# Two chunks of x held in transposed blocks until their rms is known, instead of being read a second time by rows

## The chip, the cores and the metric

One core of one Trainium2 chip. The time is device microseconds (us) of one launch, inputs in HBM to output in HBM. The kernel before takes 2092.69 us, the median of three runs (2089.51 to 2094.95).

## The reference

One decoder layer over x of 2048 positions by 1024 channels, in float32:

```python
h = rmsnorm(x, pre_norm_g)                       # x * rsqrt(mean(x*x over channels) + eps) * g
proj = h @ w_in                                  # 1024 x 8192
u_s, z_s, q, k, v, z_a, g_s, g_a = split(proj)
y_s = s5_branch(u_s, ...) * silu(z_s)
y_a = dilated_attention_branch(q, k, v) * silu(z_a)
merged = sigmoid(g_s) * (y_s @ w_branch_s) + sigmoid(g_a) * (y_a @ w_branch_a)
x = x + rmsnorm(merged @ w_out, post_norm_g)
```

Only the first line and the first use of `h` (the 512 columns of `u_s`) are touched here: the norm needs, for each position, the sum of squares over its 1024 channels.

## The kernel before

**Layout.** The products contract over channels, so the kernel keeps h transposed in SBUF: channels on the partitions in eight blocks of 128 (`k`), positions along the free axis. The 2048 positions are four chunks `q` of 512, so one block is a tile of 128x512 (256 KB). HBM holds x twice: `xT`, by chunk and block, and `x`, by rows. To keep float32 accuracy each operand is split in two float32r halves, `hi` (a ScalarE copy, L67) and `lo` (a VectorE subtraction, L68); `proj` (L132) makes one bank of 128x512 out of 24 matmuls, three for each block.

**The first stage**, `start` (L253), fills `hhi` and `hlo` and makes the four banks of `u` for each chunk (`products(q)`, L260). Two ways of handling the norm stand in it:

- Chunks 0 and 1, `load_raw` (L201): the blocks are loaded, split unscaled (L73, L74), and their squares (ScalarE, L213 and L216) are added up on VectorE (L217). Four small matmuls with a column of ones sum over the partitions (L220). The products run on the unscaled halves, and the scale goes in when a bank is evicted (L268). Later `scale_h` (L244) scales the halves for the rest of the kernel.
- Chunks 2 and 3, `rms` (L223) and then `load_scaled` (L235): the chunk is loaded by rows, four tiles `xr` of 128x1024 (512 KB, two buffers), and ScalarE squares and sums each in one instruction (L232) into `ssr` (one buffer). When the scale is known, the eight transposed blocks are multiplied by gain and scale on VectorE (L241) and split (L67, L68). The products then run on scaled halves and are evicted plainly (L266).

`spread` (L187) turns four columns of sums into the scale: a reciprocal square root out of twelve small VectorE instructions (`rsqrt`, L76, lines 80 to 90), four diagonal tiles (L194), one matmul that broadcasts them over the partitions (`bc`, L196) and a ScalarE copy into `bs` (L198, three buffers). An evicted bank `ue` goes through one of two `ev` buffers to HBM (L270).

**Order.** The program is written in the order of lines 272 to 285. The framework then fixes one order of instructions for each engine when the kernel is built, out of the program's order and a simulated timeline; on the chip each engine follows that order and waits where an operand is late. SyncE issues all these loads and stores. The blocks `xT` have seven buffers, which `scale_h` shares (its tile `ht`).

Of the kernel before, what the change touches and what calls it, by code (L numbers as in the profile page):

```python
# [11 lines left out]
F32 = mybir.dt.float32  # L12
F32R = mybir.dt.float32r
I32 = mybir.dt.int32
AF = mybir.ActivationFunctionType
ALU = mybir.AluOpType
# [3 lines left out]
D_MODEL = 1024  # L20
# [7 lines left out]
TABS = ((0, 16), (16, 16), (32, 16), (48, 16), (64, 9), (73, 9), (82, 16), (98, 16), (114, 16), (130, 16), (146, 16))  # L28
TAB_R8, TAB = 162, 163
SXB = 5  # L30


H_PAD, SHIFT = 56, 72
# [2 lines left out]
def raw(ap):  # L36
    return ap.bitcast(F32)


class Builder:  # L40
# [146 lines left out]
    def spread(self, ss, pool, psum):  # L187
# [10 lines left out]
        nc.scalar.activation(bs, bc, AF.Copy)  # L198
        return bs

    def load_raw(self, q, pool, psum, wp=None, w=None):  # L201

        nc = self.nc
        sl = slice(q * 512, (q + 1) * 512)
        acc = pool.tile([128, 512], F32, tag="xsq", name="acc", bufs=3)
        for k in range(8):
            if w and k % 2 == 0:
                self.strip(wp, w, 0, 0, slice(k, k + 2), 1)
            x = pool.tile([128, 512], F32, tag="xT", name="xT", bufs=7)
            nc.sync.dma_start(x, self.a["xT"][q, k])  # L210
            self.split(self.hhi[:, k, sl], self.hlo[:, k, sl], x, self.gpre[:, k : k + 1])
            if k == 0:
                nc.scalar.activation(acc, x, AF.Square)  # L213
            else:
                sq = pool.tile([128, 512], F32, tag="xsq", name="xsq", bufs=3)
                nc.scalar.activation(sq, x, AF.Square)  # L216
                nc.vector.tensor_tensor(acc, acc, sq, op=ALU.add)  # L217
        ss = psum.tile([128, 4], F32, tag="s", name="ss")
        for b in range(4):
            nc.tensor.matmul(ss[:, b : b + 1], acc[:, b * 128 : (b + 1) * 128], self.ones[:, 0:1], start=True, stop=True)  # L220
        return self.spread(ss, pool, psum)

    def rms(self, q, pool, psum):  # L223

        nc = self.nc
        ss = pool.tile([128, 4], F32, tag="ssr", name="ssr")
        for b in range(4):
            x = pool.tile([128, D_MODEL], F32, tag="xr", name="xr", bufs=2)
            row = q * 512 + b * 128
            nc.sync.dma_start(x, self.a["x"][row : row + 128])  # L230
            unused = pool.tile([128, D_MODEL], mybir.dt.bfloat16, tag="xsq", name="unused", bufs=3)
            nc.scalar.activation(unused, x, AF.Square, accum_out=ss[:, b : b + 1])  # L232
        return self.spread(ss, pool, psum)

    def load_scaled(self, q, bs, pool):  # L235
        nc = self.nc
        sl = slice(q * 512, (q + 1) * 512)
        for k in range(8):
            x = pool.tile([128, 512], F32, tag="xT", name="xT", bufs=7)
            nc.sync.dma_start(x, self.a["xT"][q, k])  # L240
            nc.vector.scalar_tensor_tensor(x, x, self.gpre[:, k : k + 1], bs, op0=ALU.mult, op1=ALU.mult)  # L241
            self.split(self.hhi[:, k, sl], self.hlo[:, k, sl], x)

    def scale_h(self, q, bs, pool):  # L244
        sl = slice(q * 512, (q + 1) * 512)
        for k in range(8):
            hi, lo = self.hhi[:, k, sl], self.hlo[:, k, sl]
            t = pool.tile([128, 512], F32, tag="xT", name="ht", bufs=7)
            self.nc.vector.tensor_tensor(t, raw(hi), raw(lo), op=ALU.add)
            self.nc.vector.tensor_tensor(t, t, bs, op=ALU.mult)  # L250
            self.split(hi, lo, t)

    def start(self, wp, pool, ev, psum):  # L253


        nc = self.nc
        us = [self.pair_tiles(wp) for _ in range(2)]
        back = lambda t: t.rearrange("p (s i) -> p s i", s=4)[:, ::-1]

        def products(q, scale=None):  # L260
            for ct in range(4):
                ps = psum.tile([128, 512], F32, tag=("proj", "n", "t")[(4 * q + ct) // 2 % 3], name="proj")
                self.proj(ps, us[ct // 2], ct % 2, self.pos(q))
                e = ev.tile([128, 4, 128], F32, tag="ev", name="ue")
                if scale is None:
                    nc.scalar.activation(e, back(ps), AF.Copy)  # L266
                else:
                    nc.vector.tensor_tensor(e, back(ps), back(scale), op=ALU.mult)  # L268
                s0 = 4 - 4 * (q % 2)
                nc.sync.dma_start(self.ud[ct * 128 : (ct + 1) * 128, s0 : s0 + 4, q // 2], e)  # L270

        b0 = self.load_raw(0, pool, psum, wp, us[0])
        for ct in range(1, 4):
            self.strip(wp, us[ct // 2], ct % 2, ct)
        b1 = self.load_raw(1, pool, psum)
        products(0, b0)
        b2 = self.rms(2, pool, psum)
        self.load_scaled(2, b2, pool)
        b3 = self.rms(3, pool, psum)
        self.load_scaled(3, b3, pool)  # L280
        products(1, b1)
        products(2)
        self.scale_h(0, b0, pool)
        self.scale_h(1, b1, pool)
        products(3)
# [178 lines left out]
    def ssm_pair(self, g0, pool, psum, tabd, kd):  # L464
# [68 lines left out]
        def rotation():  # L533
# [3 lines left out]
            c, s = (pool.tile(sh, F32, name=n) for n in ("rot_c", "rot_s"))  # L537
            t = pool.tile(sh, F32, tag="sx", name="rot_t", bufs=SXB)
            w = pool.tile(sh, F32, tag="sx", name="rot_w", bufs=SXB)
            g = nc.gpsimd  # L540
# [8 lines left out]
        def wide_tile():  # L549
            return pool.tile([128, 2, 256], F32, tag="sx", name="sx", bufs=SXB)  # L550

# [52 lines left out]
        def gelu():  # L604

            py = m["py"].rearrange("p g x -> p (g x)")
            v = pool.tile([128, 512], F32, tag="sx", name="gv", bufs=SXB)
            nc.scalar.activation(v, py, AF.Square)
# [686 lines left out]
```

## Time and profile before

| | |
|---|---|
| three runs | 2089.51, 2092.69 (median), 2094.95 us |
| the profiled execution | 2096.55 us, its span 2094.7 us |
| TensorE (PE) busy | 2049.4 us, 98% of the span |
| VectorE (DVE), ScalarE (ACT), GpSimd (POOL) busy | 903.0, 592.3, 397.8 us |
| read from HBM, written | 146.52 MB, 74.56 MB |

The profile is of one execution. PE is matmul, PEld its weight loads, SPq the issue of a DMA on SyncE. All times inside the profile count from the start of its span. A busy share tells how much of a time an engine worked, and not whether it was waited for; that is told by the idle time ahead of an instruction and what released it.

### The profile page before, as it was taken

The page shows a single profiled execution, that of the slowest core. Times are in us where ns is not written, and L with a number is a line of the kernel's source. Part 1 is how long each engine was busy: PE and PEld are TensorE (multiplying, and loading weights), DVE is VectorE, ACT ScalarE, POOL GpSimd, SP SyncE. Part 2 cuts the span into 40 slices and gives each one's busy share as a digit, 9 for nine tenths or more (in the row PEclk, how much of TensorE's full clock was granted, in tenths as well). Part 3 has the DMA queues.
Part 4 walks back from the last instruction along what each step waited for, and adds up shares of the span by engine and source line. Part 5 has one row for each costly group of instructions (what it writes and reads, how often), then busy time and mean ns, then how long its engine had stood idle before and what let it go on. Part 6 is the DMA issues. An engine that isn't in the chain of part 4 may idle for free.

```text
span 2094.7 us, 30801 instructions
## 1 busy us (share of the span) xinstructions
PE 2049.4 (98%) x11668; PEld 1786.1 (85%) x11668; DVE 903.0 (43%) x2261; ACT 592.3 (28%) x1327; POOL 397.8 (19%) x384
## 2 busy tenths in 40 slices
PE   8999999999999999999999999999889999999998
PEld 6788888999999988888888888887777887999997
DVE  6881355555442234324424423434311226544434
ACT  6421122222223234334434333432111124112111
POOL 0002355555521200000000000001636101111111
PEclk9999999999999999999999999999999999999999
DMA  7333333333445421111111121113757246433323
GB/s 247 116 115 140 103 115 113 118 114 113 117 121 174 152 67 57 56 61 51 61 56 56 37 66 51 61 52 118 223 157 230 88 136 201 138 125 116 117 81 101
DMA packets 208372, 231.50 MB, mean 111 GB/s; under 512 B 24864, under 2 KB 142944, under 8 KB 207968
## 3 DMA queue, kind: packets, MB, share of 16 engines
q1 hardware_dynamic: 208224, 229.54, 34.9%
q8 instruction: 91, 1.49, 0.3%
q14 instruction: 57, 0.47, 0.1%
HBM read 146.52 MB, written 74.56 MB: 106 GB/s over the span
## 4 chain that ended last, share of the span: by engine, by line
PE 86%; DMA 7%; DVE 2%; ACT 1%; POOL 1%; issue 1%; SPq 0%; DVEq 0%; ACTq 0%; POOLq 0%
PE proj L141 46%; PE pv L163 13%; PE po L1108 8%; PE br L1089 8%; DMA cf<-fd 2%; PE glu L786 2%; PE s L914 2%; PE nb L940 1%; DMA raw<-in_wout_dram 1%; PE na L940 1%; PE nc L978 1%; PE py L598 1%; POOL cn L1030 1%; PE s L970 1%; PE pd L561 1%
## 5 line engine op out<-in xcount | busy, mean ns | idle before, releaser
L141 PE MATMUL proj<-hhi,w_hi 128*128 128x512 f32 x1664 | 664.6, 400 | 25.4 <-ACT ge L693 15.6
L141 PE MATMUL proj<-hlo,w_hi 128*128 128x512 f32 x1664 | 658.2, 396 | 3.3 <-DVE hlo L68 2.7
L141 PE MATMUL proj<-hhi,w_lo 128*128 128x512 f32 x1664 | 657.5, 395 | 0.0
L141 PEld LDWEIGHTS proj<-hhi,w_hi 128*128 128x128 f32 x1664 | 314.5, 189 | 95.0 <-ACT ge L693 18.4
L141 PEld LDWEIGHTS proj<-hlo,w_hi 128*128 128x128 f32 x1664 | 314.3, 189 | 71.3 <-DVE hlo L74 3.2
L141 PEld LDWEIGHTS proj<-hhi,w_lo 128*128 128x128 f32 x1664 | 314.3, 189 | 64.8
L163 PE MATMUL pv<-w_hi,hhi 128*128 128x256 f32 x768 | 218.8, 285 | 0.0
L163 PE MATMUL pv<-w_hi,hlo 128*128 128x256 f32 x768 | 214.5, 279 | 0.0
L163 PE MATMUL pv<-w_lo,hhi 128*128 128x256 f32 x768 | 214.5, 279 | 0.0
L68 DVE TENSOR_TENSOR w_lo<-w_raw,w_hi 128x512 fp32r<-128x512 f32 (+1 forms) x130 | 107.9, 854 | 195.8 <-ACT w_hi L67 195.3
L163 PEld LDWEIGHTS pv<-w_hi,hhi 128*128 128x128 f32 x768 | 144.5, 188 | 0.6
L163 PEld LDWEIGHTS pv<-w_lo,hhi 128*128 128x128 f32 x768 | 144.4, 188 | 0.6
L163 PEld LDWEIGHTS pv<-w_hi,hlo 128*128 128x128 f32 x768 | 144.4, 188 | 0.0
L898 ACT ACTIVATE p<-p,nm 128x256 f32<-128x256 f32 (+1 forms) x192 | 89.5, 467 | 151.8 <-DVE nm L897 135.7
L892 DVE CUSTOM_DVE_ANT_0 p<-s,mask 128x256 f32<-128x256 f32 (+1 forms) x192 | 68.2, 376 | 147.1 <-PE t L973 68.8
L1092 POOL TENSOR_TENSOR gt<-gt 128x256 f32<-128x256 f32 x64 | 48.7, 763 | 390.6 <-DVE gt L1091 224.7
L67 ACT ACTIVATE w_hi<-w_raw 128x512 fp32r<-128x512 f32 (+1 forms) x130 | 76.9, 620 | 111.3 <-DMA w_raw<-in_wst_dram 72.4
L848 POOL CAST kh<-kh 128x128 fp32r<-128x128 f32 x12 | 3.6, 296 | 538.2 <-PE s L970 426.3
L1108 PE MATMUL po<-wout0h,mh 128*128 128x512 f32 x256 | 99.6, 394 | 3.3 <-ACT wout0h L67 3.3
L1108 PE MATMUL po<-wout0l,mh 128*128 128x512 f32 x256 | 100.3, 392 | 0.0
L1108 PE MATMUL po<-wout0h,ml 128*128 128x512 f32 x256 | 100.2, 393 | 0.0
L693 ACT ACTIVATE ge<-proj 128x512 f32<-128x512 f32 x64 | 37.8, 594 | 205.7 <-PE proj L141 134.3
(248 smaller groups left out, 3342.1 us busy)
## 6 DMA issues: line engine op xcount, KB each, us to landing
w_raw<-in_wst_dram SPq DMA_DIRECT2D x126, 256.0 KB
vd<-ve SPq DMA_DIRECT2D x48, 256.0 KB
numd<-acc SPq DMA_DIRECT2D x48, 256.0 KB
cn<-numd SPq DMA_DIRECT2D x48, 256.0 KB
cf<-fd SPq DMA_DIRECT2D x48, 256.0 KB
xT<-in_xT_dram SPq DMA_DIRECT2D x32, 256.0 KB
gts<-ge SPq DMA_DIRECT2D x32, 256.0 KB
sx<-sx SPq DMA_DIRECT2D x64, 128.0 KB
```

The costliest lines, as they stand in the source:

```text
L67: nc.scalar.activation(hi, src, AF.Copy)
L68: nc.vector.tensor_tensor(lo, src, raw(hi), op=ALU.subtract)
L141: last = nc.tensor.matmul(ps, st[:, k, cs], m, start=n == 0, stop=n == 23)
L163: last = nc.tensor.matmul(ps[:, o], st[:, k, rs], m[:, k], start=n == 0, stop=n == 23)
L786: nc.tensor.matmul(ps, st[:, k, cs], m[:, k], start=n == 0, stop=n == 11)
L892: nc.vector.tensor_tensor_reduce(p[:, :n], scores, mask, scale=1.0, scalar=-3.0e38, op0=ALU.add, op1=ALU.max, accum_out=st[:, 0, blk : blk ...
L898: nc.scalar.activation(p[:, :n], p[:, :n], AF.Exp, scale=HEAD_SCALE, bias=nm, accum_out=st[:, 1, blk : blk + 1])
L914: nc.tensor.matmul(s[:, h], x[:, b], y[:, k0 : k0 + 2], start=n == 0, stop=n == 2)
L940: nc.tensor.matmul(out, x, y[:, i0 : i0 + 2], start=n == 0, stop=n == 2)
L1089: nc.tensor.matmul(ps, st[:, k, cs], m[:, i, k], start=n == 0, stop=n == 11)
L1092: nc.gpsimd.tensor_tensor(gt[:, 0], gt[:, 0], gt[:, 1], op=ALU.add)
L1108: nc.tensor.matmul(po[b, half], st[:, k, bs], m[:, k, hs], start=k == 0 and n == 0, stop=k == 7 and n == 2,)
```

## The change

The loads by rows, `rms` and `load_scaled` are gone. `load_held` loads a chunk's eight transposed blocks and keeps them, takes the sum of squares as `load_raw` does (squares on ScalarE, additions on VectorE, four matmuls with ones, now the helper `column_sums`), and `split_held` then scales and splits the same blocks in place. The blocks `xT` get 11 buffers instead of seven. In SBUF the two go even: two tiles `xr` of 4 KB a partition leave, four of 2 KB come.

```diff
+XTB = 11
...
+    def column_sums(self, acc, psum):
+        ss = psum.tile([128, 4], F32, tag="s", name="ss")
+        for b in range(4):
+            block = acc[:, b * 128 : (b + 1) * 128]
+            self.nc.tensor.matmul(ss[:, b : b + 1], block, self.ones[:, 0:1], start=True, stop=True)
+        return ss
...
-    def rms(self, q, pool, psum):
-
-        nc = self.nc
-        ss = pool.tile([128, 4], F32, tag="ssr", name="ssr")
-        for b in range(4):
-            x = pool.tile([128, D_MODEL], F32, tag="xr", name="xr", bufs=2)
-            row = q * 512 + b * 128
-            nc.sync.dma_start(x, self.a["x"][row : row + 128])
-            unused = pool.tile([128, D_MODEL], mybir.dt.bfloat16, tag="xsq", name="unused", bufs=3)
-            nc.scalar.activation(unused, x, AF.Square, accum_out=ss[:, b : b + 1])
-        return self.spread(ss, pool, psum)
-
-    def load_scaled(self, q, bs, pool):
-        nc = self.nc
+        return self.spread(self.column_sums(acc, psum), pool, psum)
+
+    def load_held(self, q, pool, psum):
+
+        nc = self.nc
+        xs = []
+        acc = pool.tile([128, 512], F32, tag="xsq", name="acc", bufs=3)
+        for k in range(8):
+            x = pool.tile([128, 512], F32, tag="xT", name="xT", bufs=XTB)
+            nc.sync.dma_start(x, self.a["xT"][q, k])
+            xs.append(x)
+            if k == 0:
+                nc.scalar.activation(acc, x, AF.Square)
+            else:
+                sq = pool.tile([128, 512], F32, tag="xsq", name="xsq", bufs=3)
+                nc.scalar.activation(sq, x, AF.Square)
+                nc.vector.tensor_tensor(acc, acc, sq, op=ALU.add)
+        return xs, self.spread(self.column_sums(acc, psum), pool, psum)
+
+    def split_held(self, q, xs, bs):
         sl = slice(q * 512, (q + 1) * 512)
-        for k in range(8):
-            x = pool.tile([128, 512], F32, tag="xT", name="xT", bufs=7)
-            nc.sync.dma_start(x, self.a["xT"][q, k])
-            nc.vector.scalar_tensor_tensor(x, x, self.gpre[:, k : k + 1], bs, op0=ALU.mult, op1=ALU.mult)
+        for k, x in enumerate(xs):
+            self.nc.vector.scalar_tensor_tensor(x, x, self.gpre[:, k : k + 1], bs, op0=ALU.mult, op1=ALU.mult)
             self.split(self.hhi[:, k, sl], self.hlo[:, k, sl], x)
...
         products(0, b0)
-        b2 = self.rms(2, pool, psum)
-        self.load_scaled(2, b2, pool)
-        b3 = self.rms(3, pool, psum)
-        self.load_scaled(3, b3, pool)
+        for q in (2, 3):
+            self.split_held(q, *self.load_held(q, pool, psum))
         products(1, b1)
         products(2)
         self.scale_h(0, b0, pool)
```

## Rows read from the trace of the kernel before

**Rows 1.** The page, part 1: busy time, share of the span, instructions

```profile
PE 2049.4 (98%) x11668; PEld 1786.1 (85%) x11668; DVE 903.0 (43%) x2261; ACT 592.3 (28%) x1327; POOL 397.8 (19%) x384
```

**Rows 2.** Busy time by stretch: PE, PEld, DVE, ACT, POOL, PEclk, DMA share, GB/s

```profile
0.00:68.00 68.00, 55.14 (x221) 40.97 (x222) 44.07 (x121) 39.39 (x69) 0.85 (x7) 1.00 0.66 217
...
20.00:40.00 20.00, 20.00 (x92) 16.32 (x92) 12.12 (x32) 11.80 (x21) 0.00 (x0) 1.00 0.70 232
...
40.00:62.00 22.00, 19.65 (x82) 14.93 (x80) 11.46 (x53) 6.42 (x13) 0.00 (x0) 1.00 0.56 168
...
68.00:1400.00 1332.00, 1332.00 (x7803) 1170.69 (x7804) 593.85 (x1464) 414.03 (x956) 244.54 (x233) 1.00 0.29 90
```

**Rows 3.** Timeline of PE, 5 to 68 us: start, us, instruction [idle before, releaser]

```profile
5.57 0.80 PE L141 MATMUL proj<-hhi,w_hi 128*128 128x512 f32 x1 [5.57 <-ACT hhi L73]
...
18.24 0.95 PE L220 MATMUL ss<-ones,acc 128*128 128x1 f32 x8
...
49.36 1.10 PE L196 MATMUL bc<-diag,ones 128*128 128x512 f32 x2 [1.28 <-DVE rs_y L82]
...
62.70 1.10 PE L196 MATMUL bc<-diag,ones 128*128 128x512 f32 x2 [1.77 <-DVE diag L194]
...
67.85 0.50 PE L141 MATMUL proj<-hlo,w_hi 128*128 128x512 f32 x1 [2.70 <-DVE hlo L68]
```

**Rows 4.** Timeline of ACT, 38 to 49 us

```profile
38.05 1.06 ACT L232 ACTIVATE unused<-xr 128x1024 bf16<-128x1024 f32 x1 [3.80 <-DMA xr<-in_x_dram]
...
40.38 0.58 ACT L198 ACTIVATE bs<-bc 128x512 f32<-128x512 f32 x1
...
48.47 1.06 ACT L232 ACTIVATE unused<-xr 128x1024 bf16<-128x1024 f32 x1 [7.51 <-DVE rs_v L80]
```

**Rows 5.** Timeline of DVE, 40 to 63 us

```profile
40.99 1.29 DVE L268 TENSOR_TENSOR ue<-proj,bs 128x512 f32<-128x512 f32 x2 [6.01 <-ACT bs L198]
...
46.76 0.69 DVE L268 TENSOR_TENSOR ue<-proj,bs 128x512 f32<-128x512 f32 x1 [3.34 <-DMA ud<-ue]
...
48.23 0.16 DVE L80 TENSOR_SCALAR rs_v<-ssr 128x4 f32<-128x4 f32 x1
...
51.71 0.88 DVE L194 TENSOR_SCALAR diag<-ident,inv 128x128 f32<-128x128 f32 x4
...
62.47 4.72 DVE L241 SCALAR_TENSOR_TENSOR xT<-xT,gpre,bs 128x512 f32<-128x512 f32 x7
```

**Rows 6.** Timeline of SP: issues of loads, 30 to 70 us

```profile
30.08 0.38 SPq L240 DMA_DIRECT2D xT<-in_xT_dram  x1
...
32.68 1.40 SPq L230 DMA_DIRECT2D xr<-in_x_dram  x2
...
67.82 1.53 SPq L240 DMA_DIRECT2D xT<-in_xT_dram  x3
```

**Rows 7.** Groups by line, 0 to 230 us: busy us, mean ns

```profile
L232 ACT ACTIVATE unused<-xr 128x1024 bf16<-128x1024 f32 x8 | 8.4, 1053 | 15.6 <-DMA xr<-in_x_dram 7.9 <-DVE rs_v L80 7.5
...
L216 ACT ACTIVATE xsq<-xT 128x512 f32<-128x512 f32 x14 | 8.5, 618 | 0.5 <-DVE acc L217 0.4
...
L217 DVE TENSOR_TENSOR acc<-acc,xsq 128x512 f32<-128x512 f32 x14 | 9.6, 685 | 0.0
...
L241 DVE SCALAR_TENSOR_TENSOR xT<-xT,gpre,bs 128x512 f32<-128x512 f32 x16 | 11.0, 745 | 0.0
...
L68 DVE TENSOR_TENSOR hlo<-xT,hhi 128x512 fp32r<-128x512 f32 x16 | 10.2, 686 | 0.7 <-ACT hhi L67 0.7
```

**Rows 8.** Chain that ended last, in order of time: start, us, what

```profile
1.65 3.06 DMA xT<-in_xT_dram
...
67.85 140.83 PE proj L141 x620
```

**Rows 9.** Timelines of DVE and ACT at 88 and 89 us

```profile
88.31 0.69 DVE L68 TENSOR_TENSOR hlo<-xT,hhi 128x512 fp32r<-128x512 f32 x1
...
89.08 0.60 ACT L266 ACTIVATE ue<-proj 128x512 f32<-128x512 f32 x1 [1.22 <-PE proj L141]
```

More of the change, by code (lines that the diff above doesn't have):

```diff
@@ L217, in load_raw @@
                 nc.vector.tensor_tensor(acc, acc, sq, op=ALU.add)
-        ss = psum.tile([128, 4], F32, tag="s", name="ss")
-        for b in range(4):
-            nc.tensor.matmul(ss[:, b : b + 1], acc[:, b * 128 : (b + 1) * 128], self.ones[:, 0:1], start=True, stop=True)
-        return self.spread(ss, pool, psum)
-    def rms(self, q, pool, psum):
-        nc = self.nc
-        ss = pool.tile([128, 4], F32, tag="ssr", name="ssr")
-        for b in range(4):
-            x = pool.tile([128, D_MODEL], F32, tag="xr", name="xr", bufs=2)
-            row = q * 512 + b * 128
-            nc.sync.dma_start(x, self.a["x"][row : row + 128])
-            unused = pool.tile([128, D_MODEL], mybir.dt.bfloat16, tag="xsq", name="unused", bufs=3)
-            nc.scalar.activation(unused, x, AF.Square, accum_out=ss[:, b : b + 1])
-        return self.spread(ss, pool, psum)
-    def load_scaled(self, q, bs, pool):
-        nc = self.nc
+        return self.spread(self.column_sums(acc, psum), pool, psum)
+    def load_held(self, q, pool, psum):
+        nc = self.nc
+        xs = []
+        acc = pool.tile([128, 512], F32, tag="xsq", name="acc", bufs=3)
+        for k in range(8):
+            x = pool.tile([128, 512], F32, tag="xT", name="xT", bufs=XTB)
+            nc.sync.dma_start(x, self.a["xT"][q, k])
[8 more added lines that the diff above has]
+    def split_held(self, q, xs, bs):
         sl = slice(q * 512, (q + 1) * 512)
-        for k in range(8):
-            x = pool.tile([128, 512], F32, tag="xT", name="xT", bufs=7)
-            nc.sync.dma_start(x, self.a["xT"][q, k])
-            nc.vector.scalar_tensor_tensor(x, x, self.gpre[:, k : k + 1], bs, op0=ALU.mult, op1=ALU.mult)
+        for k, x in enumerate(xs):
+            self.nc.vector.scalar_tensor_tensor(x, x, self.gpre[:, k : k + 1], bs, op0=ALU.mult, op1=ALU.mult)
             self.split(self.hhi[:, k, sl], self.hlo[:, k, sl], x)
@@ L247, in scale_h @@
             hi, lo = self.hhi[:, k, sl], self.hlo[:, k, sl]
-            t = pool.tile([128, 512], F32, tag="xT", name="ht", bufs=7)
+            t = pool.tile([128, 512], F32, tag="xT", name="ht", bufs=XTB)
             self.nc.vector.tensor_tensor(t, raw(hi), raw(lo), op=ALU.add)
```

## The prediction, made before the changed kernel was run

> **What bounds the kernel now.** I read the page's busy times first. TensorE is busy for 2049.4 us of a span of 2094.7 [rows 1]: whatever shortens this kernel has to take idle time, or work, away from TensorE. Next the busy time by stretch, to see where that idle time lies [rows 2]. From 68 to 1400 us TensorE is busy for all of 1332 us, and the chain of waits runs over TensorE alone from 67.85 us, 620 matmuls of `proj` in 140.83 us, 0.227 us each [rows 8]. So a microsecond that the first 68 us gain or lose goes straight through to the end: behind them stands a line of matmuls without a hole. In the first 68 us TensorE is busy for 55.14 us and idle for 12.86 us [rows 2]. That is the whole stake.
>
> The timeline of TensorE says what the 12.86 us are [rows 3]. The first 5.57 us are the wait for the first block, which the change doesn't touch. Three more waits are large: 1.28 us ahead of the matmul that broadcasts chunk 1's scale, 1.77 us ahead of chunk 3's, and 2.70 us for the first `lo` half of chunk 2. Together they are 5.75 us; what is left, 12.86 - 5.57 - 5.75 = 1.54 us, is small waits in the first 20 us.
>
> Then I asked why the scales come late, on ScalarE and VectorE. ScalarE stood still for 3.80 us until rows of chunk 2 landed, and the copy `bs` of chunk 0, which needs no rows, stood behind them in ScalarE's order until 40.38 us [rows 4]. The first eviction on VectorE waited 6.01 us for this copy, a later one 3.34 us for a store to free an `ev` buffer [rows 5]. Chunk 2's reciprocal square root stands behind those evictions, so it starts at 48.23 us, though ScalarE was done with chunk 2's rows when it made that copy at 40.38; ScalarE's next square, the first of chunk 3, waits 7.51 us for the root's first step, since `ssr` has one buffer [rows 4, 5]. VectorE reaches chunk 2's first scaled block at 62.47 us. Call this time T; TensorE's wait of 2.70 us follows from it.
>
> **The change, part by part.**
>
> *Removed.* Eight row loads of 512 KB with their issues on SyncE [rows 6]; eight squares with sums on ScalarE, 8 x 1.053 = 8.4 us [rows 7]; the single buffer `ssr`; and the point at which rows block ScalarE ahead of chunk 0's copy. TensorE executed none of it.
>
> *Added on ScalarE.* 16 squares of a block, 16 x 0.618 = 9.9 us [rows 7], 1.5 us more than leaves. ScalarE is busy for 6.42 of the 22 us from 40 to 62 [rows 2], so I cost it at nothing; without that cover it is 1.5 us.
>
> *Added on VectorE.* 14 additions x 0.685 = 9.6 us [rows 7]. VectorE is idle for 7.9 us of 20 to 40 and 10.5 us of 40 to 62 [rows 2], and chunk 2's additions, 4.8 us, fall there. Chunk 2's scaling and splitting, 8 x (0.745 + 0.686) = 11.4 us [rows 7], moves forward into the same idle time. Cost zero on TensorE while it fits; if it does not, the ends to take are zero and 9.6 us.
>
> *Added on TensorE.* Two sets of small matmuls with ones at 0.95 us [rows 3]: 1.9 us. This is paid in full, since there is no hole to hide it in.
>
> *Moved: T.* The seventh block of chunk 2 is issued at 30.08 us already; the eighth has to wait until 67.82 us for a buffer [rows 6]. With 11 buffers it follows at about 30.5 us, and lands 0.38 + 3.06 us later [rows 6, 8], at 33.9 us. Then a square (0.62), an addition (0.69), the sums (0.95), the reciprocal square root to the end of the diagonals (48.23 to 52.59, 4.36 us), the broadcast (1.10) and the copy (0.58) [rows 3, 4, 5, 7] come to 8.3 us. So T is 42.2 us at the earliest, and at the latest the 62.47 us of now. I take 47, near the lower end: of what lies between, the waits for rows and for `ssr` go, while a store's wait like the 3.34 us and two evictions (1.3 us) can still stand ahead.
>
> *The wait that the change adds.* Chunk 2 holds eight of 11 blocks, so five blocks of chunk 3 can be loaded only when a `lo` of chunk 2 frees theirs; chunk 3's scale now hangs on chunk 2's split. Queued behind these loads on SyncE are stores of `u`, behind the squares on ScalarE the `hi` copies. After the last `lo` of chunk 2, T + 11.4, come load (3.4), square and addition (1.3), sums (0.95), the root (4.36), broadcast and copy (1.7): chunk 3's scale is there at T + 23.2 and its last `lo` at T + 34.6, which is 81.6 us. Before, that `lo` started at 88.31 us, and the last bank of chunk 2 was evicted at 89.08 [rows 9]. A bank takes 24 x 0.227 = 5.45 us, and its last block is read 4.8 us in, at 93.9; with the gain below, 91.8. There are 10 us to spare, so I cost this at nothing.
>
> *The three waits.* The 2.70 us go, since chunk 2 is split before TensorE wants it (about 60 us). The 1.28 us go, since chunk 0's copy no longer stands behind rows. The 1.77 us I leave in: chunk 3's chain is still the last and got longer, and a broadcast that follows a small chain is what waited. The new sums may wait too; the nearest rows are the broadcasts' waits, 0 to 1.77 us each [rows 3], and I take 0, nearest to the existing sums, which sit between matmuls without a wait worth a row.
>
> **The sum** is -2.70 - 1.28 + 1.9 = -2.1 us. The profiled execution took 2096.55 us, 3.9 us above the median of 2092.69; the sum comes off either. **Forecast: 2090.6 us**, -0.1%. A measurement of this kernel can tell about 0.3%, 6.3 us, from no change.
>
> **A rule that speaks against the change.** The change takes away DMA and ScalarE time and gives TensorE work, though TensorE is the engine at 98% [rows 1]. The Trainium skill, Perfetto Trace Analysis, section Identifying the Most-Contended Engine, says to optimize the engine of highest occupancy first; taken alone it would leave only the 1.9 us here. The trace disagrees for this stage, where TensorE waited 5.75 us on others. The case itself is the first rival.
>
> **Rivals.**
>
> *The waits form again.* The orders are fixed at build time, and a broadcast or a sum stands in TensorE's order wherever the simulated timeline put it. The three waits come back elsewhere, at the same 5.75 us, and the sums add 1.9: 2094.6 us. For it: four scales and now four sums hang on chains of small VectorE instructions, and VectorE gets fuller. Against: the 2.70 us come from T alone, which moves by 15 us.
>
> *Chunk 3 in lockstep: slower.* Its place is ScalarE's order. If the five late squares stand between chunk 2's `hi` copies, each waits for a load that waits for a `lo`, and the next copy waits behind it. A round is `lo` 0.69, issue 0.38, landing 3.06, square 0.62, copy about 0.62, together 5.4 us in place of 1.43; five rounds add 19.7 us. Chunk 3's last `lo` falls at 101.3 us instead of 81.6, 9.5 us after TensorE wants it, and -2.1 + 9.5 = +7.4 gives 2100.1 us. It costs from the point at which chunk 3 is over 10 us late. For it: the 3.80 us with an unrelated copy behind them are this very pattern [rows 4]. Against: in program order chunk 2's split stands ahead of chunk 3's loads. That ScalarE takes its queue strictly in order is in the Trainium skill, TensorE: Matmul & The Clock Gate, section Architectural detail; [rows 4] agree.
>
> *Everything goes.* All 5.75 us and the 1.54 us of small waits, since the early loads no longer share the DMA queue with rows: -7.3 + 1.9 = -5.4, 2087.3 us. Against: none of the waits of TensorE that have a row was released by a load [rows 3].
>
> **How the numbers follow.** The forecast 0.47, waits form again 0.20, lockstep 0.20, everything goes 0.13. The range runs from 2087.3 less half the spread of the runs (2.7), 2084.5, to the lockstep, 2100.5. Faster by over 0.3% is below 2086.4, which even the best case reaches only with the spread's help: 0.10. Slower by over 0.3% is above 2099.0, most of the lockstep: 0.16. Within: 0.74.
>
> **What would show it.** Right: T near 47 us; TensorE idle in the first 68 us down from 12.86 to about 9; no wait for a `lo` at chunk 2; two more rows of four sums at 0.95 us; still no hole from the first product of chunk 2 to 1400 us. Wrong: T above 57 us, TensorE waiting for chunk 3's `lo`, ScalarE idle for DMA between `hi` copies, or holes past 68 us, where the sum puts none.

## The result, and the profile of the changed kernel

The changed kernel takes 2121.29 us, the median of four runs (2120.79 to 2122.2), beside 2091.64 us for the kernel before on the same chip: a ratio of 1.0138, 95% interval 1.0123 to 1.0153. The forecast was 2090.6 us and its range ended at 2100.5. The profiled execution took 2122.2 us and its span is 2120.4, beside 2094.7 before, so 25.7 us of span have to be found. (The medians are 29.7 us apart; the profiled execution of the kernel before was 4.9 us above its median.)

The page of the changed kernel, busy time, share of the span and instructions, answers to [rows 1]:

```profile
PE 2062.1 (97%) x11684; PEld 1795.0 (85%) x11684; DVE 914.5 (43%) x2275; ACT 594.6 (28%) x1327; POOL 399.9 (19%) x384
```

The busy shares are those of before to a point. TensorE has 16 instructions more, the new sums, and is busy for 12.7 us longer; the sums explain 1.9 of that.

To place the loss I took a landmark, the first matmul of the next stage (`pk`). The kernel before reaches it at 208.51 us, the changed one at 234.09:

```profile
234.09 0.51 PE L509 MATMUL pk<-tab,q 128*128 128x16 f32 x4
```

That is 25.6 us, the whole difference of the spans. So between these two executions nothing is lost or won behind the first stage, and only the first 234 us need reading. Busy time by stretch of the changed kernel (columns as in [rows 2]):

```profile
0.00:68.00 68.00, 55.86 (x228) 42.46 (x229) 49.32 (x117) 37.90 (x65) 0.85 (x7) 0.96 0.54 175
...
68.00:100.00 32.00, 24.06 (x99) 19.37 (x98) 31.45 (x62) 13.07 (x22) 0.00 (x0) 0.87 0.24 74
...
100.00:110.00 10.00, 3.50 (x5) 1.67 (x6) 8.50 (x19) 4.47 (x8) 0.00 (x0) 0.50 0.02 5
...
100.00:150.00 50.00, 41.00 (x160) 31.99 (x161) 41.27 (x183) 15.49 (x26) 0.00 (x0) 0.83 0.33 101
...
150.00:1400.00 1250.00, 1250.00 (x7420) 1102.36 (x7419) 514.61 (x1207) 378.63 (x885) 247.14 (x233) 1.00 0.28 88
```

TensorE's first 68 us hardly changed: idle for 12.14 us, against 12.86 before. The chain that ended last, in order of time (answers to [rows 8]), has the unbroken run of matmuls from 113.16 us, where before it was from 67.85:

```profile
113.16 121.09 PE proj L142 x524
```

The loss lies where the kernel before had no hole at all: 7.94 us idle between 68 and 100, 9.00 between 100 and 150. Idle time of TensorE in the first 150 us is 29.1 us, 16.2 more than before. In the same stretches the granted clock is below 1, down to 0.50 between 100 and 110, which is the lower of TensorE's two levels, 1.2 GHz of 2.4. And VectorE, 43% busy over the span, worked for 31.45 of the 32 us from 68 to 100. The waits of TensorE from 0 to 250 us (waited for, us in total, times, longest):

```profile
PE bc L197 <- DVE diag L195: 12.3, 1, 12.3
PE proj L142 <- ACT hhi L74: 6.7, 2, 5.8
PE proj L142 <- DVE hlo L69: 5.2, 2, 2.7
PE proj L142 <- ACT hhi L68: 4.3, 2, 2.1
```

One wait is three quarters as long as all the extra idle time: 12.3 us for the diagonals of chunk 3's scale. The second row is the first load and was there before. TensorE's timeline (answers to [rows 3]):

```profile
51.98 1.02 PE L197 MATMUL bc<-diag,ones 128*128 128x512 f32 x2
52.83 0.95 PE L206 MATMUL ss<-ones,acc 128*128 128x1 f32 x8
...
59.42 1.02 PE L197 MATMUL bc<-diag,ones 128*128 128x512 f32 x2
62.58 1.84 PE L142 MATMUL proj<-hhi,w_hi 128*128 128x512 f32 x4 [2.13 <-ACT hhi L68]
67.16 0.80 PE L142 MATMUL proj<-hlo,w_hi 128*128 128x512 f32 x1 [2.74 <-DVE hlo L69]
67.75 0.63 PE L142 MATMUL proj<-hhi,w_lo 128*128 128x512 f32 x1
...
85.96 0.95 PE L206 MATMUL ss<-ones,acc 128*128 128x1 f32 x8
...
104.37 2.08 PE L197 MATMUL bc<-diag,ones 128*128 128x512 f32 x2 [12.31 <-DVE diag L195]
108.58 2.08 PE L142 MATMUL proj<-hhi,w_hi 128*128 128x512 f32 x4 [2.13 <-ACT hhi L68]
113.16 0.80 PE L142 MATMUL proj<-hlo,w_hi 128*128 128x512 f32 x1 [2.50 <-DVE hlo L69]
```

The rows are, in this order, chunk 1's broadcast, chunk 2's sums and broadcast, then chunk 3's sums and broadcast. The last two broadcasts are each followed by the same pair of waits: 2.1 us until the scale is copied and the first block is scaled and copied, then 2.5 to 2.7 us until the first `lo` is there. Behind both pairs the matmuls run at half speed for a while: 12 of them from 67.75 us and eight from 113.75 start 0.427 us apart, where 0.227 is the rule.

The cause is one engine further back. VectorE's timeline of the changed kernel (answers to [rows 5]):

```profile
61.11 5.39 DVE L248 SCALAR_TENSOR_TENSOR xT<-xT,gpre,bs 128x512 f32<-128x512 f32 x8 [0.80 <-ACT bs L199]
66.42 4.89 DVE L69 TENSOR_TENSOR hlo<-xT,hhi 128x512 fp32r<-128x512 f32 x8
71.23 0.68 DVE L242 TENSOR_TENSOR acc<-acc,xsq 128x512 f32<-128x512 f32 x1
71.84 1.89 DVE L256 TENSOR_TENSOR ht<-hhi,hlo 128x512 f32<-128x512 f32 x3
...
88.13 0.15 DVE L81 TENSOR_SCALAR rs_v<-ss 128x4 f32<-128x4 f32 x1
88.20 1.28 DVE L257 TENSOR_TENSOR ht<-ht,bs 128x512 f32<-128x512 f32 x2
89.41 0.16 DVE L83 TENSOR_SCALAR rs_y<-rs_v 128x4 int32<-128x4 int32 x1
89.48 0.68 DVE L69 TENSOR_TENSOR hlo<-ht,hhi 128x512 fp32r<-128x512 f32 x1
...
101.57 0.15 DVE L91 SCALAR_TENSOR_TENSOR inv<-rs_t,rs_n 128x4 f32<-128x4 f32 x1
...
103.45 0.86 DVE L195 TENSOR_SCALAR diag<-ident,inv 128x128 f32<-128x128 f32 x4
...
107.11 5.39 DVE L248 SCALAR_TENSOR_TENSOR xT<-xT,gpre,bs 128x512 f32<-128x512 f32 x8 [0.81 <-ACT bs L199]
112.42 4.89 DVE L69 TENSOR_TENSOR hlo<-xT,hhi 128x512 fp32r<-128x512 f32 x8
```

Read the tile names. The tile `ht` belongs to `scale_h`, which rescales chunks 0 and 1 for stages that come much later. Its steps of 0.68 us stand between chunk 3's additions, and again between the twelve small steps of chunk 3's square root: 24 of them between 88.13 us and the diagonals at 103.45, one every 0.60 us. The root and its diagonals take 16.2 us. VectorE waits for nothing there, so the list of waits leads to the diagonals and no further; VectorE is busy with work that nobody needs yet, while TensorE stands still for the one small chain in its midst.

**The account of the 25.6 us**: 16.2 us more idle time; 1.9 us for the new sums; and half-speed work, 20 matmuls x 0.200 = 4.0, the broadcast 2.08 - 1.10 = 1.0, two groups of four at 1.84 and 2.08 where 1.20 is the full-speed time (it stands in a row further down) = 1.5, together 6.5 us. The sum is 24.6; 1.0 us is left over.

**The kernel before had a small case of this already.** This is VectorE's timeline in its trace at chunk 3's root, which no row ahead of the prediction shows:

```profile
57.62 0.16 DVE L87 TENSOR_TENSOR rs_t<-rs_y 128x4 f32<-128x4 f32 x1
57.69 1.28 DVE L268 TENSOR_TENSOR ue<-proj,bs 128x512 f32<-128x512 f32 x2
58.89 0.15 DVE L88 TENSOR_TENSOR rs_t<-rs_t,rs_v 128x4 f32<-128x4 f32 x1
...
61.68 0.87 DVE L194 TENSOR_SCALAR diag<-ident,inv 128x128 f32<-128x128 f32 x4
```

Two evictions stand between two steps of the root. In that kernel the root was over at 62.55 us, ahead of `scale_h`, whose first step came at 82.2. Now the busy time of the kernel before from 68 to 100 us (columns as in [rows 2]):

```profile
68.00:100.00 32.00, 32.00 (x142) 26.48 (x143) 31.30 (x52) 13.26 (x23) 0.00 (x0) 1.00 0.39 124
```

VectorE was full there before the change too, 31.30 of 32 us. The change pushed chunk 3's whole chain into that stretch.

### The profile page after: what moved, and what is told of

Its sections match the earlier page's. It is cut to its first block, busy times and chain, and to the rows that moved or that the text cites. A ratio compares the mean times of both kernels' runs of the same rounds, so it can differ in the third digit from the quotient of the medians.

```text
span 2120.4 us, 30842 instructions
## 1 busy us (share of the span) xinstructions
PE 2062.1 (97%) x11684; PEld 1795.0 (85%) x11684; DVE 914.5 (43%) x2275; ACT 594.6 (28%) x1327; POOL 399.9 (19%) x384
## 4 chain that ended last, share of the span: by engine, by line
PE 90%; DMA 5%; DVE 3%; POOL 1%; ACT 1%; issue 0%; SPq 0%; DVEq 0%; POOLq 0%; ACTq 0%
PE proj L142 49%; PE pv L164 13%; PE po L1113 8%; PE br L1094 8%; DMA cf<-fd 2%; PE glu L791 2%; PE s L919 2%; PE nb L945 1%; PE na L945 1%; DMA cn<-numd 1%; PE nc L983 1%; PE py L603 1%; POOL cn L1035 1%; PE s L975 1%; PE pd L566 1%; PE py L602 1%
## 5 line engine op out<-in xcount | busy, mean ns | idle before, releaser
L69 DVE TENSOR_TENSOR w_lo<-w_raw,w_hi 128x512 fp32r<-128x512 f32 (+1 forms) x130 | 113.7, 897 | 218.4 <-ACT w_hi L68 218.1
L903 ACT ACTIVATE p<-p,nm 128x256 f32<-128x256 f32 (+1 forms) x192 | 89.5, 467 | 148.7 <-DVE nm L902 132.4
```

The costliest lines, as they stand in the source:

```text
L69: nc.vector.tensor_tensor(lo, src, raw(hi), op=ALU.subtract)
L903: nc.scalar.activation(p[:, :n], p[:, :n], AF.Exp, scale=HEAD_SCALE, bias=nm, accum_out=st[:, 1, blk : blk + 1])
```

## The experiments

All compute everything. In the edits, `issue_after(x)` queues what the block issues on the engine of x behind x in that engine's order; it adds no wait between engines. The ratio is to the kernel before on the same chip. "Landmark" is the start of the first `pk` matmul in the profiled execution. Behind it the profiled executions take 1876.8 to 1886.3 us, though no edit touches the later stages, so the landmark shows the first stage without that scatter.

| version | median us (runs) | ratio, 95% interval | landmark us |
|---|---|---|---|
| before | 2091.64 to 2093.21 | 1 | 208.51 |
| the change | 2121.29 (4) | 1.0138, 1.0123 to 1.0153 | 234.09 |
| A. both rescalings queued | 2098.2 (10) | 1.0034, 1.0021 to 1.0046 | 214.31 |
| B. one rescaling queued | 2105.36 (4) | 1.0064, 1.0044 to 1.0084 | 220.39 |
| C. chunk 3's blocks read twice | 2103.79 (4) | 1.0067, 1.0046 to 1.0087 | 224.19 |
| D. only chunk 2 held | 2095.34 (10) | 1.0016, 1.0003 to 1.0029 | 212.26 |
| E. only chunk 3 held | 2098.65 (6) | 1.0036, 1.0022 to 1.0050 | 216.62 |
| F. before, rescalings queued | 2092.32 (10) | 1.0003, 0.9989 to 1.0017 | 207.36 |
| G. A and lagged scaling | 2095.53 (10) | 1.0023, 1.0013 to 1.0033 | 210.28 |
| H. A and evictions queued | 2099.59 (6) | 1.0045, 1.0028 to 1.0062 | 219.47 |
| I. A, lag and evictions | 2091.7 (10) | 1.0008, 0.9998 to 1.0017 | 208.68 |
| J. I and an order on TensorE | 2093.7 (12) | 1.0006, 0.9995 to 1.0016 | 210.46 |

**A. Both rescalings queued behind chunk 3's last split on VectorE.** Nothing else in the program differs from the change; the framework plans the orders of all engines anew.

```diff
+        with self.tc.issue_after(last.ins):
             self.scale_h(0, b0, pool)
             self.scale_h(1, b1, pool)
```

> The changed kernel, with the two scalings of chunks 0 and 1 (scale_h) queued on VectorE behind chunk 3's last split; loads, buffers and sums are as changed. Theory A (the steps of scale_h that the planner puts between the steps of chunk 3's root stretch it from 4.4 to 16 us, and TensorE's wait of 12.3 us for the broadcast hangs on that): the root takes 4 to 5 us again, the 12.3 us wait goes, and with it the two waits of 2.1 and 2.5 us behind it and the slow matmuls that follow them; 2097 to 2103 us. Theory B (the five blocks of chunk 3 that wait for buffers come too late, whatever the order): the broadcast is still waited for by 8 us or more; 2113 to 2122 us.

2098.2 us: 23 of the 30 us come back through an order alone, and 19.8 of the 25.6 us at the landmark. VectorE at chunk 3's root in this kernel:

```profile
79.76 0.16 DVE L81 TENSOR_SCALAR rs_v<-ss 128x4 f32<-128x4 f32 x1 [4.08 <-PE ss L206]
...
82.01 0.87 DVE L195 TENSOR_SCALAR diag<-ident,inv 128x128 f32<-128x128 f32 x4
```

The root with its diagonals takes 3.1 us in place of 16.2, and the broadcast, at 87.67 us, waits for nothing. Three waits of TensorE are left: 2.13 us for chunk 2's first `hi`, then 3.38 and 2.36 us for the first `lo` of chunks 2 and 3 (the last had been expected to go). The loads and the work on every engine are those of the change, so neither the DMA traffic nor the additions by themselves are what cost 23 us. TensorE's order moved too: chunk 3's sums stand at 78.78 us in place of 85.96. A alone therefore can't separate the length of the root from its start; B can.

**B. Only one of the two rescalings queued**, for a dose in between.

```diff
         self.scale_h(0, b0, pool)
-        self.scale_h(1, b1, pool)
+        with self.tc.issue_after(last.ins):
+            self.scale_h(1, b1, pool)
```

> The changed kernel with only one of the two rescalings (scale_h of chunk 1) queued behind chunk 3's last split on VectorE; that of chunk 0 is left as free as it was. Theory A (steps of scale_h that stand between the root's small steps on VectorE make chunk 3's scale late): eight pairs of steps of chunk 0 are left, most of them are used up between chunk 3's additions, so that about three to five stand between the root's steps. The root with its diagonals then takes 5 to 8 us in place of 16, the broadcast of chunk 3 starts at 94 to 97 us in place of 104.4, and the time is 2107 to 2113 us, between that of the order alone (2098) and that of the change (2121). Rival: it is not the steps between, but that the root begins late, at 88 us; then the root begins at the same place and the time stays within 3 us of 2121. Rival 2: any one of the two rescalings is free of cost, and the time is that of the order alone, 2098.

2105.36 us, 1.6 below the band expected of theory A, 13 below the first rival's band and 7 above the second rival's time. The broadcast, expected at 94 to 97 us, starts at 92.31. VectorE's timeline at the root:

```profile
87.27 0.15 DVE L81 TENSOR_SCALAR rs_v<-ss 128x4 f32<-128x4 f32 x1
87.34 0.68 DVE L258 TENSOR_TENSOR ht<-ht,bs 128x512 f32<-128x512 f32 x1
...
91.38 0.87 DVE L195 TENSOR_SCALAR diag<-ident,inv 128x128 f32<-128x128 f32 x4
```

and TensorE's behind it:

```profile
92.31 1.13 PE L197 MATMUL bc<-diag,ones 128*128 128x512 f32 x2 [0.51 <-DVE diag L195]
95.57 1.59 PE L142 MATMUL proj<-hhi,w_hi 128*128 128x512 f32 x4 [2.13 <-ACT hhi L68]
```

This is the cleanest pair with the change: the root begins 0.9 us from where it began there, but three steps of `ht` stand in it instead of 24, and it takes 5.0 us instead of 16.2. TensorE's wait for the diagonals falls from 12.31 to 0.51 us. So the length of the root, and not its late start alone, is what TensorE waited for. The rest, 6.1 us at the landmark between A and B, goes with the start, still 7.5 us behind A: 3.3 us more of waits, and most of what is left is more matmuls at half speed.

**C. Chunk 3 squared from blocks that are not kept, and read a second time for the split.** Its loads no longer hang on chunk 2's split.

```diff
-        for q in (2, 3):
-            self.split_held(q, *self.load_held(q, pool, psum))
+        self.split_held(2, *self.load_held(2, pool, psum))
+        _, b = self.load_held(3, pool, psum)
+        self.load_scaled(3, b, pool)
```

> The changed kernel, but chunk 3's squares are taken from blocks that are let go at once, and the blocks are loaded a second time for the split, so that its sums wait for no buffer of chunk 2. Theory A: scale_h's steps still stand between the root's steps, so the root still takes 13 us or more, but it begins some 20 us earlier and ends before TensorE is through with chunk 2's products; the 12.3 us wait is under 3 us; 2097 to 2105 us. Theory B: the wait goes too, 2097 to 2103 us. A third theory, that the added sums themselves (additions and small matmuls) cost the time wherever they stand: 2113 us or more.

2103.79 us, which rules out the third theory; theories A and B expected nearly the same time. The rescalings are not queued here, and the root is the longest of all, but starts 19 us earlier. VectorE's timeline:

```profile
69.08 0.15 DVE L81 TENSOR_SCALAR rs_v<-ss 128x4 f32<-128x4 f32 x1
...
88.61 0.88 DVE L195 TENSOR_SCALAR diag<-ident,inv 128x128 f32<-128x128 f32 x4
```

and TensorE's:

```profile
92.86 1.02 PE L197 MATMUL bc<-diag,ones 128*128 128x512 f32 x2
96.28 1.20 PE L142 MATMUL proj<-hhi,w_hi 128*128 128x512 f32 x4 [2.40 <-ACT hhi L68]
102.66 0.79 PE L142 MATMUL proj<-hlo,w_hi 128*128 128x512 f32 x1 [5.19 <-DVE hlo L69]
```

The root takes 20.4 us (chunk 2's eight `lo` stand in it beside the steps of `ht`) and TensorE does not wait for it, since it is over by 89.5. So there are two conditions: a root in the midst of filler, and one that starts late. The late start has causes of its own in the change. One is the five blocks of chunk 3 that wait for a free buffer. SyncE's timeline in the changed kernel (answers to [rows 6]):

```profile
67.13 2.73 SPq L235 DMA_DIRECT2D xT<-in_xT_dram  x5
```

The first goes out behind chunk 2's first `lo`, at 67.13 us. C is still 15.7 us behind the kernel before at the landmark. TensorE waits 6.3 us ahead of chunk 2's products, and 2.40 and 5.19 us ahead of chunk 3's, whose scalings begin at 94.81 us, after the broadcast, and whose first `lo` comes at 101.91, behind eight scalings and three more steps of `ht`.

**D and E. Only one of the two chunks held**, the other by rows as before (nine buffers for the blocks, one for the rows, so that SBUF holds both).

```diff
-        for q in (2, 3):
-            self.split_held(q, *self.load_held(q, pool, psum))
+        self.split_held(2, *self.load_held(2, pool, psum))
+        b = self.rms(3, pool, psum)
+        self.load_scaled(3, b, pool)
```

> Chunk 2 held, chunk 3 by rows as before (nine block buffers and one row buffer, to fit). If chunk 3's place behind chunk 2's buffers is the cause, chunk 2's half of the change costs its sums, 0.9 us, and what slow matmuls follow its waits, up to 3 us: 2091 to 2097 us. If holding a chunk costs by itself: half of the 30 us, 2103 to 2109 us.

> Chunk 2 by rows as before, chunk 3 held (nine block buffers and one row buffer). Chunk 3's blocks wait for chunk 2's buffers here too, and scale_h's steps stand between the additions and the root's steps in VectorE's order: if these two are the cause, TensorE waits for chunk 3's broadcast by 8 us or more, 2110 to 2124 us. If holding a chunk costs by itself: 2103 to 2109 us.

D takes 2095.34 us, as expected, E 2098.65. E misses what was expected of it by over 11 us. Its trace agrees with the mechanism, though: in E the framework put only five steps of `ht` between the root's first step and the diagonals, and the root takes 5.8 us (81.24 to 87.07). TensorE's waits there are 2.14 us for the diagonals, 2.91 and 3.11 behind it. Over the 3.1 us of A, the roots of B, E and the change (three, five and 24 steps) are longer by 0.54 to 0.63 us for each step. The two parts of the change lose 0.16% and 0.36% by themselves and 1.38% together; they don't add up. The filler that lands in the root, five steps here and 24 there, is a result of the whole order; the fewer buffers of D and E may have a part in it, which no run separates.

**F. The kernel before with the same queueing as A.**

> The kernel before with the same queue alone: scale_h behind chunk 3's last split on VectorE. There the root of chunk 3 is through before any step of scale_h is ready, so by theory A (the steps between the root's steps) the queue has nothing to win: the first 150 us stay as they are, 2090 to 2095 us. If queueing scale_h late is a gain or a loss of its own, which would then be part of what the same queue did for the changed kernel: outside 2088 to 2097 us.

2092.32 us, no difference that can be told. The rescalings did not harm the kernel before, so what A gains is a repair of something the change brought.

**G, H, I. What is left after A.** G lets `split_held` scale block k only behind the `lo` of block k - 2; in the change all eight scalings stand ahead of the first `lo` (61.11 and 107.11 us). H queues chunk 1's evictions behind chunk 2's last split. I does both.

```diff
+            with self.tc.issue_after(lo[k - 2].ins) if k >= 2 else nullcontext():
                 self.nc.vector.scalar_tensor_tensor(x, x, self.gpre[:, k : k + 1], bs, ...)
...
+        with self.tc.issue_after(first.ins):
             products(1, b1)
```

> The changed kernel with scale_h queued as before, and in each split the scaling of block k queued on VectorE behind the lo of block k-2, in place of eight scalings and then eight subtractions. The first lo comes 3 us earlier (some 63.5 us instead of 66.8), so the wait of 3.4 us for it goes to under 1 us, chunk 3's wait of 2.4 us likewise, and chunk 2's buffers come free from then on: 2093 to 2097 us. If TensorE only meets the next block too late instead (1.43 us of VectorE for a block against 0.68 us of matmuls in one bank), the wait is split over the blocks and nothing is won: 2097 to 2100 us.

> The changed kernel with scale_h queued as before, and the evictions of chunk 1's products queued on VectorE behind chunk 2's last split. Chunk 2's root then follows chunk 1's directly instead of standing behind two evictions that wait for chunk 1's scale and for a store: the first scaled block (61.5 us now) at 55 to 57 us, the waits of 2.1 and 3.4 us ahead of chunk 2 down to 1 to 2 us, and with less waiting no slow matmuls: 2092 to 2096 us. If the place of the evictions doesn't set that time, or the evictions held back stop TensorE for want of a bank: 2098 us or more.

> All three orders together: scale_h behind chunk 3's split, chunk 1's evictions behind chunk 2's split, and scaling and subtraction by turns. Chunk 2's first lo at about 58 us, before TensorE is through with chunk 1 (60 us): no wait above 1 us between 20 and 200 us, no slow matmul after the first 15 us. What is left against the kernel before is -5.75 us of waits and +1.9 us of sums: 2087 to 2091 us. If a cost of holding the blocks is left that no order takes away: 2094 us or more.

G, 2095.53 us, removes both waits for a `lo`; two waits of 2.13 and 2.14 us for a first `hi` stay. H gains nothing over A, 2099.59 us, a miss: its first scaled block comes at 61.34 us, not at 55 to 57, it keeps the bunched scalings, and its waits for `lo` are 3.84 and 3.36 us. I, 2091.7 us, is back at the time of the kernel before, 0.7 above the band expected of it. The waits of TensorE in it that belong to chunks 2 and 3, from 0 to 250 us:

```profile
PE proj L142 <- ACT hhi L68: 2.1, 1, 2.1
...
PE proj L142 <- DVE hlo L69: 0.4, 2, 0.2
```

and VectorE's timeline at chunk 2's scale:

```profile
54.13 0.16 DVE L81 TENSOR_SCALAR rs_v<-ss 128x4 f32<-128x4 f32 x1 [5.00 <-PE ss L206]
...
61.42 1.42 DVE L250 SCALAR_TENSOR_TENSOR xT<-xT,gpre,bs 128x512 f32<-128x512 f32 x2 [4.17 <-ACT bs L199]
```

2.56 us of waits are left of 5.75, the clock is at 1.00 from 20 to 150 us, and the landmark is 0.2 us behind that of before: of the 3.2 us won, the sums take 1.9, and 0.95 went in the first 20 us, of which TensorE was busy for 12.07 against 13.02 before; that leaves 0.5 us unexplained. With these orders the change is worth nothing that can be measured.

I also shows what holds T, the first scaled block of chunk 2. The evictions no longer stand ahead, and VectorE now waits 5.00 us for chunk 2's sums, which have their place in TensorE's order. The diagonals end at 57.26; the broadcast has its place at 59.73, without a wait of TensorE.

**J. As I, with an order on TensorE too**: chunk 1's third bank behind chunk 2's sums, its fourth behind chunk 2's broadcast.

```diff
+        behind = {2: self.ss, 3: self.bc}
...
-                self.proj(ps, us[ct // 2], ct % 2, self.pos(q))
+                with self.tc.issue_after(behind[ct].ins) if ct in behind else nullcontext():
+                    self.proj(ps, us[ct // 2], ct % 2, self.pos(q))
```

> The version with the three orders on VectorE (rescalings, lag of the scalings, evictions of chunk 1 behind chunk 2's split), and with one on TensorE more: the third bank of chunk 1 stands behind chunk 2's four small matmuls of sums, the fourth behind chunk 2's broadcast. Theory (what holds T, VectorE's first scaled block of chunk 2, at 61.4 us in every version that holds chunk 2 is TensorE's own fixed order, in which the sums and the broadcast stand behind chunk 1's matmuls): T comes to 54 to 58 us, the last wait for a hi of chunk 2 (2.13 us at 62.9) goes, and the time is 2088 to 2092 us, 0.999 to 1.000 of the kernel before. Rival: T is held by VectorE, and TensorE now stands still itself ahead of the sums or of the broadcast, for 1 to 5 us; then the time is 2093 to 2097.

2093.7 us. The ratio alone can't tell the theory (0.999 to 1.000) from its rival, but the trace shows the rival's wait: the 2.13 us are gone, and TensorE now stands still ahead of chunk 1's broadcast. Its timeline:

```profile
50.22 2.00 PE L197 MATMUL bc<-diag,ones 128*128 128x512 f32 x2 [2.56 <-DVE diag L195]
52.01 1.71 PE L206 MATMUL ss<-ones,acc 128*128 128x1 f32 x8
53.57 0.77 PE L142 MATMUL proj<-hhi,w_hi 128*128 128x512 f32 x1
54.15 0.63 PE L142 MATMUL proj<-hlo,w_hi 128*128 128x512 f32 x1
```

T is 62.50 us. Chunk 2's broadcast follows the third bank, at 60.81, though its diagonals end at 56.86. I and J sit one bank apart (5.45 us) and have T within 1.1 us of each other: with matmuls ordered by whole banks, TensorE either meets the small chain too late or waits for it. A cut inside a bank wasn't tried, nor were more buffers for the blocks of chunk 3. No version beats the kernel before.

## Why the prediction was wrong

**The bound was read rightly.** All that the first stage lost went through to the end, 25.6 of 25.7 us between the two profiled executions.

**"There are 10 us to spare, so I cost this at nothing" failed**, and with it the sum. It was the term of chunk 3's chain, and three of its links were wrong:
- *The root at 4.36 us* [rows 5]. It measured 16.2 us. I took a duration from where the root stands among evictions and moved it to a stretch where VectorE has other work queued. A and B show this link: 3.1 us without filler, 5.0 with three steps, 16.2 with 24.
- *T at 47 us.* It measured 61.11. The waits for rows and for `ssr` did go, and the limits behind them took over. None of chunk 2's squares waits for a load, but ScalarE's squares and VectorE's additions wait for each other in turn, one block in 1.39 us, where the prediction took one square and one addition behind the last load: the additions end at 44.41 us, not at 35.2. Then the sums have their place in TensorE's order at 52.83. Chunk 2's root begins at 54.87 behind evictions, and once these are moved (I) it waits for the sums, and the scaling for a broadcast, which TensorE's order puts at 53 to 60 us. What TensorE's own order would make late next was not asked.
- *From T to the start of the root, 17.05 us.* It measured 88.13 - 61.11 = 27.0: the additions are interleaved with `ht`, and the sums stand at 85.96 in TensorE's order. A, without the filler, has 79.76 - 61.48 = 18.3, of which 4.08 are a wait for the sums that the prediction did not have.

Together the three links were put 11.8 + 14.1 + 10.0 = 35.9 us too low, and chunk 3's last `lo`, put at 81.6 us, ended at 117.3, far beyond the 10 us to spare.

**The cover was looked for in the wrong stretch.** "VectorE is idle for 7.9 us of 20 to 40 and 10.5 us of 40 to 62" is true, and chunk 2's additions fell there (34.82 to 44.41 us); its scaling and splitting, from 61.11 us, did not. Chunk 3's additions and root, by the prediction's own chain, fall behind T + 11.4, and there VectorE was busy for 31.30 of 32 us. That row was never read; [rows 2] have one row for 68 to 1400, in which it vanishes.

**The three waits.** The 1.28 us went, but not for the reason given, so this term was right by luck. Chunk 0's copy now stands behind chunk 2's squares in ScalarE's order and runs at 41.64 us, later than the 40.38 of before [rows 4], and chunk 1's diagonals end at 49.68 us, no earlier than before (49.21). What changed is the place of chunk 1's broadcast in TensorE's order: 51.98 us in place of 49.36 [rows 3]. The 2.70 us did not go: 2.74 us stand at the same place, with 2.13 ahead of them. The 1.77 us that were left in became 12.31.

**The sums, 1.9 us, were right**: four rows of 0.95 us in place of two, none with a wait. ScalarE's extra 1.5 us cost TensorE no wait that a row shows, though the squares had their part in T.

**Half speed was not in the sum.** The waits brought TensorE's clock down twice, 6.5 us.

**The range.** Its upper end is stated as the lockstep's time, which the prediction's own sum puts at 2100.1 us and not at 2100.5. The measured time lies over 20 us above either.

**The rivals.** The lockstep of chunk 3 came nearest: chunk 3 late by more than its 10 us, holes past 68 us. Its engine was wrong. It expected loads between ScalarE's copies; the trace has the eight copies of chunk 2 in one run from 61.90 us, ahead of the late squares, and none waits for a load. That kind of strict order was cited for ScalarE, and it was VectorE's that decided. The Trainium skill, Perfetto Trace Analysis, section Identifying the Most-Contended Engine, says to optimize the engine of highest occupancy first, and to judge TensorE by its FLOPs or by the busy share of its weight loads. By the weight loads it is TensorE here (85%, VectorE 43%), and the trace agrees that TensorE's time counts; but what moved it by 23 us was another order of VectorE's work (A).

**The signs named in advance were good.** T above 57, a wait for chunk 3's `lo` and holes past 68 us were listed as what would show the sum wrong, and all three are in the trace.

## What to carry to other kernels

Before a chain of small instructions is moved, list what its engine will have ready to run at the new place, stretch by stretch: where orders are fixed when the kernel is built, big steps with no urgency can stand between the small ones, and no wait of that engine will show it. Cost such a chain by the steps that can stand in it, and give the urgent chain its place by queueing the filler behind it. And when a late operand is made early, ask where the consumer's own order has it: here TensorE's place for a broadcast, and not the data, set the next limit.

## What the runs showed of the hardware

TensorE's clock fell to the lower of its two levels behind pauses of 2 to 3 us, and not behind each of that size. In the change it was at 0.59 of full speed from 62.5 to 64.5 us, in the four matmuls behind the wait of 2.13 us, and at 0.50 from there to 73; the second fall came within the 12.31 us. In J it fell behind 2.56 us alone (0.54 from 50 to 53). In G a wait of 2.14 us left it at 1.00 (62.86 to 64.1), and behind one of 2.13 us it was at 0.50 (88.9 to 90.8). In the kernel before, 1.77 and 2.70 us with a few matmuls between left it at 1.00 [rows 2, 3], and so did 2.55 us at chunk 2 in E and 2.36 us at chunk 3 in A. So the length of a single pause does not decide it; what does stays open. In the change the two falls cost 12 and eight matmuls at 0.427 us in place of 0.227, 2.4 and 1.6 us, and with the slower matmuls ahead of these 6.5 us in all.
